# Seven-product chunks of the down projection: product order, order of the sums, and which chunks use them

## The chip, the cores and the metric

One core of one Trainium2 chip. The number is the device time in microseconds (us) of one launch. The kernel before takes 1178.64 us, the median of 3 runs (1177.26 to 1179.37).

## The reference

One decoder layer on x of 256 tokens by 2048 features, all in float32:

```
proj = x @ W_in                                   # 2048 x 6144
a    = diff_attention(...), b = moba_attention(...)
h    = LayerNorm(alpha * x + concat(a, b) @ W_out)
u    = h @ W_up                                   # 2048 x 11264: gate g and value v, 5632 each
act  = silu(conv_b + causal_conv3(g)) * v         # 256 x 5632
out  = LayerNorm(alpha * h + act @ W_down)        # W_down: 5632 x 2048
```

Only the last product, act @ W_down, and the second LayerNorm's sums are touched by the change.

## The kernel before, in words

Every float32 operand of a matmul is split into a rounded part `hi` (ScalarE copies it to fp32r) and a rest `lo` (VectorE subtracts). A product is then three matmuls: hi by hi, hi by lo, lo by hi. Weights come as a stream of chunks of 128 x 2048 numbers (1 MB) through four buffers `raw`; chunk i + 6 is loaded by SyncE's queue when chunk i begins (`load`). `begin(i)`, `middle(i)` and the matmuls of chunk i are written out chunk after chunk, and each engine runs its own instructions in just that order. So the text of `begin` and `middle` is the queue of ScalarE (ACT) and VectorE (DVE): `begin(i)` prepares chunk i + 2 (second half) and the activations of i + 1 and i + 2, `middle(i)` prepares the first half of chunk i + 3.

The down projection runs in two column passes n = 0 and 1, each over 22 chunks p (two of the 44 rows-of-128 of W_down, 1024 of its columns). The chunk is a 2 x 2 block problem: the two 128-token halves t, the two row blocks k, the two blocks c of 512 columns. A normal chunk (`mm_d`) makes 8 block products of three matmuls with 512 columns, 24 matmuls, into four PSUM banks `CB[t][c]`. A seven-product chunk (`mm_seven`, a Strassen-Winograd form) makes 7 block products, 21 matmuls. It needs sums of activation blocks (`act_sums`, split in `act_sums_split` into `sh`, `sl`) and of weight blocks, and its split weights lie in one tile `slot` of 7 blocks: blocks 0 to 2 are raw (unsummed), blocks 3 to 6 are sums. The rest of blocks 0 to 2 is made by ACT writing the negative rounded part and then a DMA from POOL's queue that adds the raw numbers on top (`blocks_raw`, line 517). Blocks 3 and 4 get their rest in `blocks_lo`, blocks 5 and 6 in `blocks_sum`. Four products go to banks of their own, `MB[1], MB[5], MB[6], MB[7]`, which are added to the result z once a pass in `shared_out`.

Before, the seven-product chunks (`SEVEN`, line 45) are p = 2, 5, 8, 11, 14, 17, 20 in pass 0 and 1, 4, 7, 10, 13, 16 in pass 1: 13 in all, two normal chunks between any two. The tile `slot` exists once. The split activations `ah, al` (k = 0) and `bh, bl` (k = 1) have so few buffers that the copies at the head of `begin(i)` wait until the matmuls of chunk i - 1 are done.

The last four chunks of pass 1 (`last`) aren't run chunk by chunk: they go column block by column block, so that LayerNorm can begin early. Two of them have split weights in tiles of their own, `end0` and `end1`, made in the bodies of the two chunks ahead (lines 906 to 916). `gb` (2 MB, scale and offset of the last LayerNorm) is loaded at p = 9 of pass 1 (line 905). At the end of pass 0 the banks `CB` are added to z by `z_piece`, which also takes the LayerNorm statistics of each piece (line 400), at lines 924 to 934; the next pass writes the same banks.

Of the kernel before, what the change touches and what calls it, by code (L numbers as in the profile page):

```python
# [11 lines left out]
F32 = mybir.dt.float32  # L12
F32R = mybir.dt.float32r
AF = mybir.ActivationFunctionType
ALU = mybir.AluOpType

P = 128
D = 2048
# [11 lines left out]
ALPHA = 2.0 ** 0.25  # L30
# [11 lines left out]
PAIRED_END = 4  # L42
PT = FT // 2

SEVEN = (range(2, PT, 3), range(1, PT - PAIRED_END, 3))

ENDS = {(1, 1): ("cos_d", "sin_d"), (2, 0): ("mask", "cos_m"), (2, 1): ("sin_m", "lam4")}

# [2 lines left out]
def hymba_layer(ctx: ExitStack, tc: tile.TileContext, a: dict):  # L51
# [72 lines left out]
    def split(i, half, both=None):  # L124

        if i >= NS or (i, half) in parts:
            return
        t = loaded[i] if half == 0 else loaded.pop(i)
        if both is None:
            hi = splits.tile([P, 1024], F32R, name="hi")  # L130
            lo = splits.tile([P, 1024], F32R, name="lo")
        else:
            hi, lo = both[:, half], both[:, 2 + half]
        for x, y in pieces(i, half):
            if i < 4 and x % 512 == 0:
                split_x(4 * i + x // 512, 4 * i + (y + 511) // 512)
            s = slice(x - 1024 * half, y - 1024 * half)
            ACT.activation(hi[:, s], t[:, x:y], AF.Copy)  # L138
            DVE.tensor_tensor(lo[:, s], t[:, x:y], hi[:, s].bitcast(F32), ALU.subtract)  # L139
        parts[i, half] = (hi, lo)  # L140
# [101 lines left out]
    def at(step, fn, *args, rank=LATER):  # L242
        after.setdefault(step, []).append((rank, len(after.get(step, ())), fn, args))
# [210 lines left out]
    def seven(i):  # L454
        return stream[i][0] == "d" and stream[i][1] in SEVEN[stream[i][2]]

# [16 lines left out]
    def split_act(i, k):  # L473

        if i >= NS or stream[i][0] != "d" or (i, k) in aparts:
            return
        src = act_of(2 * stream[i][1] + k)
        hi, lo = act_tiles(i, k)
        ACT.activation(hi, src, AF.Copy)
        DVE.tensor_tensor(lo, src, hi.bitcast(F32), ALU.subtract)  # L480
        aparts[i, k] = (hi, lo)
# [5 lines left out]
    def act_sums(i):  # L487
        p = stream[i][1]
        x = [act_of(2 * p + k) for k in range(2)]
        a11, a21, a12, a22 = (x[k][:, t * P:(t + 1) * P] for k in range(2) for t in range(2))  # L490
        f = [keep.tile([P, 2, P], F32, name="sf", tag=g) for g in ("cos_d", "sin_d")]
        DVE.tensor_tensor(f[0][:, 0], a21, a11, ALU.subtract)
        DVE.tensor_tensor(f[0][:, 1], a22, a21, ALU.subtract)
        DVE.tensor_tensor(f[1][:, 0], f[0][:, 1], a11, ALU.add)
        DVE.tensor_tensor(f[1][:, 1], a12, f[1][:, 0], ALU.subtract)
        sums[i] = f

    def act_sums_split(i):
        f = sums[i]
        out = []  # L500
        for j in range(2):
            hi = keep.tile([P, 2, P], F32R, name="sh", tag=("mask", "cos_m")[j])
            lo = keep.tile([P, 2, P], F32R, name="sl", tag=("sin_m", "lam4")[j])
            ACT.activation(hi, f[j], AF.Copy)  # L504
            DVE.tensor_tensor(lo, f[j], hi.bitcast(F32), ALU.subtract)
            out += [(hi[:, k], lo[:, k]) for k in range(2)]

        sums[i] = out
# [3 lines left out]
    def blocks_raw(i):  # L512

        t = loaded[i].rearrange("p (b c) -> p b c", c=512)
        slot = keep.tile([P, 2, 7, 512], F32R, name="slot", tag="t2")
        ACT.activation(slot[:, 1, 0:3], t[:, 0:3], AF.Copy, scale=-1.0)
        POOL.dma_start(slot[:, 1, 0:3], t[:, 0:3], accum_op=ALU.add)
        f = [work.tile([P, 512], F32, name="tf", tag="m1") for _ in range(2)]
        DVE.tensor_tensor(f[0], t[:, 0], t[:, 3], ALU.subtract)
        DVE.tensor_tensor(f[1], t[:, 3], t[:, 2], ALU.add)  # L520
        blocks[i] = (slot, f)
        for j in range(2):
            ACT.activation(slot[:, 0, 3 + j], f[j], AF.Copy)
        ACT.activation(slot[:, 0, 0:3], t[:, 0:3], AF.Copy)

    def blocks_lo(i):
        slot, f = blocks[i]
        for j in range(2):
            DVE.tensor_tensor(slot[:, 1, 3 + j], f[j], slot[:, 0, 3 + j].bitcast(F32), ALU.subtract)  # L529

    def blocks_sum(i, j):

        t = loaded[i].rearrange("p (b c) -> p b c", c=512)
        slot, f = blocks[i]
        DVE.tensor_tensor(f[0], t[:, 2 - j], f[0], ALU.subtract)  # L535
        ACT.activation(slot[:, 0, 5 + j], f[0], AF.Copy)  # L536
        DVE.tensor_tensor(slot[:, 1, 5 + j], f[0], slot[:, 0, 5 + j].bitcast(F32), ALU.subtract)
        if j == 1:
            loaded.pop(i)


    idle = keep.tile([P, 512], mybir.dt.bfloat16, name="idle")
# [12 lines left out]
    def begin(i):  # L555

        urgent(i)
        j = i + 2
        split_act(j - 1, 1)
        split_act(j, 0)  # L560
        if j < NS and seven(j):
            blocks_raw(j)
        else:
            split(j, 1)
        if j - 1 < NS and seven(j - 1):
            blocks_sum(j - 1, 1)
            act_sums_split(j - 1)
        load(i + 6)
        pending(i)

    def middle(i):

        urgent(i + 0.5)
        if i + 2 < NS and seven(i + 2):
            blocks_lo(i + 2)
            act_sums(i + 2)
            blocks_sum(i + 2, 0)
        if i + 3 < NS and not seven(i + 3):
            split(i + 3, 0)
        pending(i + 0.5)  # L580

# [264 lines left out]
    def mm_seven(i):  # L846
        n = stream[i][2]
        slot, _ = blocks.pop(i)
        s3, s1, s2, s4 = sums.pop(i)
        (h0, l0), (h1, l1) = aparts[i, 0], aparts[i, 1]  # L850
        a11, a12, a22 = (h0[:, 0:P], l0[:, 0:P]), (h1[:, 0:P], l1[:, 0:P]), (h1[:, P:], l1[:, P:])
        for m, lhs, b in ((5, s1, 3), (7, s3, 4), (6, s2, 5), (1, a11, 0), (2, a12, 1), (3, s4, 2), (4, a22, 6)):
            t, c = {2: (0, 0), 3: (0, 1), 4: (1, 0)}.get(m, (None, None))
            key, dst = ((n, m), MB[m]) if t is None else ((n, t, c), CB[t][c])
            if m == 6:
                middle(i)
            mm_three(key, dst, lhs, (slot[:, 0, b], slot[:, 1, b]))

    def z_add(n, t, c, src, alpha=1.0):
        s = slice((2 * n + c) * 512, (2 * n + c + 1) * 512)  # L860
        DVE.scalar_tensor_tensor(z[:, t, s], z[:, t, s], alpha, src, op0=ALU.mult, op1=ALU.add)  # L861

    def shared_out(n):

        u = acts[2][:, 12:14].rearrange("p a b -> p (a b)")
        ACT.activation(u, MB[1], AF.Copy)
        z_add(n, 0, 0, u, ALPHA)
        DVE.tensor_tensor(u, MB[6], u, ALU.add)
        z_add(n, 0, 1, MB[5], ALPHA)
        z_add(n, 0, 1, u)  # L870
        DVE.tensor_tensor(u, MB[7], u, ALU.add)
        z_add(n, 1, 1, MB[5], ALPHA)
        z_add(n, 1, 0, u, ALPHA)
        z_add(n, 1, 1, u)

    last = range(NS - PAIRED_END, NS)

# [23 lines left out]
    for i in range(first_d, NS - PAIRED_END):  # L901
        begin(i)
        _, p, n, _ = stream[i]
        if n == 1 and p == 9:
            load_gb(2, keep.tile([P, 2, D], F32, name="gb2", tag="ma"))
        if i == last[0] - 2:
            end1 = keep.tile([P, 4, 1024], F32R, name="end1", tag="mb")
            split(last[3], 0, end1)
            split(last[3], 1, end1)
        if i == last[0] - 1:  # L910
            end0 = keep.tile([P, 4, 1024], F32R, name="end0", tag="t2")
            split(last[2], 0, end0)
            split(last[2], 1, end0)
            for j in last[1:]:
                for k in range(2):
                    split_act(j, k)
        if seven(i):
            mm_seven(i)
            if p == SEVEN[n][-1]:
                at(i + 1, shared_out, n)  # L920
        else:
            for k in range(2):
                mm_d(i, 0, [0, 1], k)
            if n == 0 and p == PT - 1:
                for c in range(2):
                    z_piece(0, c, CB[0][c], 2, alpha=1.0)
            if i < last[0] - 1:
                middle(i)
            for k in range(2):
                mm_d(i, 1, [0, 1], k)  # L930
            done(i)
            if n == 0 and p == PT - 1:
                for c in range(4):
                    z_piece(1, c, CB[1][c // 2][:, c % 2 * 256:c % 2 * 256 + 256], 2, 256, 1.0)
        for k in range(2):
            aparts.pop((i, k))

# [132 lines left out]
```

## Time and profile before

| | |
|---|---|
| median of 3 runs | 1178.64 us |
| profiled execution's own time | 1178.97 us |
| its span in the trace | 1177.1 us |
| granted clock of TensorE, mean | 0.986 |
| first matmul of the down projection | 888.33 us |
| last matmul | 1165.95 us |

Times in the rows are microseconds from the start of the span. PE is TensorE (PEld its weight loads), DVE VectorE, ACT ScalarE, POOL GpSimd, SP SyncE (with a q behind the name: its queue). A timeline row is: start, length, engine, line, operation, the tile written and the tiles read, shapes, how many instructions are merged (x2), and in brackets the idle time of the engine just before and what ended it. Matmuls overlap in the pipeline, so the step from one start to the next is what a matmul costs, not its length; DVE and ACT instructions overlap by about 0.1 us in the same way.

### The profile page before, as it was taken

How to read it: one execution, taken by the hardware profiler on the slowest of the kernel's cores; microseconds unless marked ns; L12 is line 12 of the kernel's file. 1: busy time of each engine (PE TensorE's matmuls, PEld its weight loads, DVE VectorE, ACT ScalarE, POOL GpSimd, SP SyncE). 2: the span in 40 equal slices, each digit the busy share in tenths (PEclk: the TensorE clock that was granted, in tenths of full speed). 3: DMA queues.
4: the chain of work that ended last, by engine and by line, in shares of the span. 5: the costliest groups of instructions: out<-in, count | busy, mean ns of one | idle time of the engine just before them, and what ended most of it. 6: DMA issues, size and time to landing. Idle time of an engine off the chain costs nothing.

```text
span 1177.1 us, 15646 instructions
## 1 busy us (share of the span) xinstructions
PE 1136.3 (97%) x5965; PEld 962.7 (82%) x5965; DVE 822.5 (70%) x1399; ACT 622.7 (53%) x1019; POOL 32.0 (3%) x40
## 2 busy tenths in 40 slices
PE   9999999999999999999999999999999999789976
PEld 6888888888888888888888888888887777567755
DVE  6886877858646777776566666666667877777774
ACT  6565555444434565455454455455456666456641
POOL 0000000000000000000000000000000000000004
PEclk9999999999999999999999999999999999889988
DMA  9665454444555285555554555555556778467921
GB/s 340 256 242 181 157 179 173 159 171 178 179 178 184 103 321 182 202 189 179 197 195 181 190 200 183 184 200 189 183 185 199 209 217 259 142 188 215 330 81 72
DMA packets 47611, 228.13 MB, mean 194 GB/s; under 512 B 4656, under 2 KB 6576, under 8 KB 27952
## 3 DMA queue, kind: packets, MB, share of 16 engines
q1 hardware_dynamic: 45664, 216.92, 51.9%
q0 software_dynamic: 1872, 10.22, 4.3%
q8 instruction: 46, 0.75, 0.3%
q14 instruction: 29, 0.24, 0.1%
HBM read 214.80 MB, written 2.10 MB: 184 GB/s over the span
## 4 chain that ended last, share of the span: by engine, by line
PE 87%; DVE 6%; issue 2%; ACT 2%; DMA 1%; SPq 0%; POOL 0%; ACTq 0%; DVEq 0%
PE bank L206 87%; DVE lo L139 2%; ACT hi L138 1%; DVE tf L535 1%; DVE z L861 1%; DMA raw<-in_w_d 1%; DVE bl L480 0%; PE bank L329 0%; DVE al L480 0%; DMA raw<-in_w_v 0%; ACT sh L504 0%; DVE end L139 0%; DVE st L400 0%; DVE z L397 0%; DVE slot L529 0%
## 5 line engine op out<-in xcount | busy, mean ns | idle before, releaser
L139 DVE TENSOR_TENSOR lo<-raw,hi 128x1024 fp32r<-128x1024 f32 (+1 forms) x368 | 436.0, 1200 | 206.8 <-ACT hi L138 206.3
L138 ACT ACTIVATE hi<-raw 128x1024 fp32r<-128x1024 f32 (+1 forms) x368 | 375.9, 1034 | 214.6 <-PE bank L206 187.0
L206 PE MATMUL bank<-h,hi 128*128 128x512 f32 x1376 | 477.2, 390 | 0.0
L206 PE MATMUL bank<-h,lo 128*128 128x256 f32 x1376 | 388.0, 282 | 0.0
L206 PEld LDWEIGHTS bank<-h,hi 128*128 128x128 f32 x1376 | 258.3, 188 | 54.1
L206 PEld LDWEIGHTS bank<-h,lo 128*128 128x128 f32 x1376 | 260.1, 189 | 0.0
L206 PE MATMUL bank<-x,hi 128*128 128x512 f32 x512 | 181.6, 396 | 0.0
L206 PE MATMUL bank<-x,lo 128*128 128x256 f32 x512 | 144.3, 282 | 0.0
L206 PEld LDWEIGHTS bank<-x,hi 128*128 128x128 f32 x512 | 96.1, 188 | 21.7 <-issue 1.3
L206 PEld LDWEIGHTS bank<-x,lo 128*128 128x128 f32 x512 | 96.8, 189 | 0.2
L206 PE MATMUL bank<-hi,x 128*128 128x512 f32 x256 | 85.3, 402 | 0.7 <-ACT hi L138 0.7
L206 PEld LDWEIGHTS bank<-hi,x 128*128 128x128 f32 x256 | 48.1, 188 | 13.2 <-ACT hi L138 1.9
L443 ACT ACTIVATE gc<-gs,vec 128x256 f32<-128x256 f32 x43 | 25.9, 602 | 58.6 <-DVE gs L220 58.6
L206 PE MATMUL bank<-lo,x 128*128 128x512 f32 x128 | 50.8, 397 | 0.4 <-DVE lo L139 0.4
L206 PE MATMUL bank<-hi,ah 128*128 128x512 f32 (+1 forms) x118 | 39.2, 404 | 9.6 <-DVE z L397 9.6
L536 ACT ACTIVATE slot<-tf 128x512 fp32r<-128x512 f32 x26 | 16.4, 632 | 55.1 <-DVE tf L535 55.1
L206 PE MATMUL bank<-slot,sh 128*128 128x512 f32 x104 | 35.0, 419 | 9.6 <-ACT sh L504 9.6
L446 ACT ACTIVATE gc<-gc 128x256 f32<-128x256 f32 x44 | 18.4, 418 | 48.9 <-DVE gc L445 48.9
L206 PE MATMUL bank<-hi,mh 128*128 128x512 f32 x128 | 42.1, 400 | 0.0
L206 PE MATMUL bank<-lo,mh 128*128 128x512 f32 x128 | 41.6, 395 | 0.0
L206 PE MATMUL bank<-hi,ml 128*128 128x512 f32 x128 | 41.6, 395 | 0.0
L444 DVE SCALAR_TENSOR_TENSOR gc<-gs,vec,gc 128x255 f32<-128x255 f32 x43 | 20.8, 484 | 28.8 <-ACT gc L443 28.8
(176 smaller groups left out, 1355.8 us busy)
## 6 DMA issues: line engine op xcount, KB each, us to landing
raw<-in_w_u SPq DMA_DIRECT2D x88, 1024.0 KB, 4.8
raw<-in_w_d SPq DMA_DIRECT2D x88, 512.0 KB, 5.3
raw<-in_w_qk SPq DMA_DIRECT2D x32, 1024.0 KB, 4.9
raw<-in_w_o SPq DMA_DIRECT2D x16, 1024.0 KB, 4.8
raw<-in_w_v SPq DMA_DIRECT2D x12, 1024.0 KB, 4.8
slot<-raw POOLq DMA_DIRECT2D x13, 768.0 KB, 6.5
raw<-in_w_v SPq DMA_DIRECT2D x8, 256.0 KB, 4.7
raw<-in_w_v SPq DMA_DIRECT2D x4, 512.0 KB, 7.6
```

What stands on the lines that cost most here:

```text
L138: ACT.activation(hi[:, s], t[:, x:y], AF.Copy)
L139: DVE.tensor_tensor(lo[:, s], t[:, x:y], hi[:, s].bitcast(F32), ALU.subtract)
L206: PE.matmul(out, lhsT, rhs, start=start, stop=stop)
L443: ACT.activation(gc, g, AF.Identity, bias=vec[:, C_CB + f:C_CB + f + 1], scale=w[2])
L444: DVE.scalar_tensor_tensor(gc[:, 1:], g[:, 0:S - 1], w[1], gc[:, 1:], op0=ALU.mult, op1=ALU.add)
L446: ACT.activation(gc, gc, AF.Silu)
L535: DVE.tensor_tensor(f[0], t[:, 2 - j], f[0], ALU.subtract)
L536: ACT.activation(slot[:, 0, 5 + j], f[0], AF.Copy)
L861: DVE.scalar_tensor_tensor(z[:, t, s], z[:, t, s], alpha, src, op0=ALU.mult, op1=ALU.add)
```

## The change

The set of seven-product chunks becomes p = 3, 6, 9, 12, 15, 18 in pass 0 and 1, 4, 7, 10, 13 in pass 1: 11 instead of 13. Within such a chunk the products of raw block 0 and raw block 1 come first. For a seven-product chunk c the preparation is laid out anew: in `begin(c-2)` the activation sums follow `blocks_raw`; in `middle(c-2)` the order is rest of block 3, sum for block 5, rest of block 4, split of the activation sums, rounded block 5, first half of chunk c + 1, rest of block 5; in `begin(c-1)` it is sum for block 6, second half of chunk c + 1, rounded block 6, rest of block 6. `shared_out` is cut in two, run one and two chunks after the last seven-product chunk of the pass. At the end of pass 0 the banks are added to z in whole 512-column pieces without statistics, and the statistics (`z_stats`) follow in `begin` of chunks 1 and 2 of pass 1. The own tiles of the two last chunks are both made in the body of the chunk just ahead of the last four.

```
-SEVEN = (range(2, PT, 3), range(1, PT - PAIRED_END, 3))
+SEVEN = (range(3, 19, 3), range(1, 14, 3))
...
-    def blocks_lo(i):
+    def blocks_lo(i, *js):
         slot, f = blocks[i]
-        for j in range(2):
-            DVE.tensor_tensor(slot[:, 1, 3 + j], f[j], slot[:, 0, 3 + j].bitcast(F32), ALU.subtract)
+        for j in js:
+            DVE.tensor_tensor(slot[:, 1, 3 + j], f[j % 2 if j < 2 else 0], slot[:, 0, 3 + j].bitcast(F32),
+                              ALU.subtract)
...                                                             # blocks_sum(i, j):
         DVE.tensor_tensor(f[0], t[:, 2 - j], f[0], ALU.subtract)
-        ACT.activation(slot[:, 0, 5 + j], f[0], AF.Copy)
-        DVE.tensor_tensor(slot[:, 1, 5 + j], f[0], slot[:, 0, 5 + j].bitcast(F32), ALU.subtract)
         if j == 1:
             loaded.pop(i)
+
+    def blocks_hi(i, j):
+        slot, f = blocks[i]
+        ACT.activation(slot[:, 0, 5 + j], f[0], AF.Copy)
...                                                             # begin(i), j = i + 2:
         if j < NS and seven(j):
             blocks_raw(j)
+            act_sums(j)
+        elif j - 1 < NS and seven(j - 1):
+            blocks_sum(j - 1, 1)
+            split(j, 1)
+            blocks_hi(j - 1, 1)
+            blocks_lo(j - 1, 3)
         else:
             split(j, 1)
-        if j - 1 < NS and seven(j - 1):
-            blocks_sum(j - 1, 1)
-            act_sums_split(j - 1)
...                                                             # middle(i):
         if i + 2 < NS and seven(i + 2):
-            blocks_lo(i + 2)
-            act_sums(i + 2)
+            blocks_lo(i + 2, 0)
             blocks_sum(i + 2, 0)
-        if i + 3 < NS and not seven(i + 3):
+            blocks_lo(i + 2, 1)
+            act_sums_split(i + 2)
+            blocks_hi(i + 2, 0)
+            split(i + 3, 0)
+            blocks_lo(i + 2, 2)
+        elif i + 3 < NS and not seven(i + 3):
             split(i + 3, 0)
...                                                             # mm_seven:
-        for m, lhs, b in ((5, s1, 3), (7, s3, 4), (6, s2, 5), (1, a11, 0), (2, a12, 1), (3, s4, 2), (4, a22, 6)):
+        for m, lhs, b in ((1, a11, 0), (2, a12, 1), (5, s1, 3), (7, s3, 4), (6, s2, 5), (3, s4, 2), (4, a22, 6)):
...
+    def shared_out(n, part):
         u = acts[2][:, 12:14].rearrange("p a b -> p (a b)")
+        if part == 0:
+            ACT.activation(u, MB[1], AF.Copy)
+            z_add(n, 0, 1, MB[5], ALPHA)
+            z_add(n, 1, 1, MB[5], ALPHA)
+            z_add(n, 0, 0, u, ALPHA)
+            DVE.tensor_tensor(u, MB[6], u, ALU.add)
+        else:
+            z_add(n, 0, 1, u)
+            DVE.tensor_tensor(u, MB[7], u, ALU.add)
+            z_add(n, 1, 0, u, ALPHA)
+            z_add(n, 1, 1, u)
...                                                             # the loop over chunks:
-        if i == last[0] - 2:
-            end1 = keep.tile([P, 4, 1024], F32R, name="end1", tag="mb")
-            split(last[3], 0, end1)
-            split(last[3], 1, end1)
         if i == last[0] - 1:
-            end0 = keep.tile([P, 4, 1024], F32R, name="end0", tag="t2")
-            split(last[2], 0, end0)
-            split(last[2], 1, end0)
-            for j in last[1:]:
+            split_act(last[1], 1)
+            for j, g in ((last[2], "t2"), (last[3], "mb")):
+                end = keep.tile([P, 4, 1024], F32R, name="end", tag=g)
                 for k in range(2):
                     split_act(j, k)
+                    split(j, k, end)
...
             if p == SEVEN[n][-1]:
-                at(i + 1, shared_out, n)
+                at(i + 1, shared_out, n, 0)
+                at(i + 2, shared_out, n, 1)
...                                                             # p = 21 of pass 0, ahead of middle(i):
-                    z_piece(0, c, CB[0][c], 2, alpha=1.0)
+                    z_add(0, 0, c, CB[0][c])
...                                                             # and behind its matmuls:
-                for c in range(4):
-                    z_piece(1, c, CB[1][c // 2][:, c % 2 * 256:c % 2 * 256 + 256], 2, 256, 1.0)
+                for c in range(2):
+                    z_add(0, 1, c, CB[1][c])
+                for t in range(2):
+                    for c in range(2):
+                        at(i + 2 + t, z_stats, t, c, (512, 256)[t])
```

`z_stats(t, c, w)` runs the `bn_stats` instructions of one piece of 512 columns, in widths w.

## Rows read from the trace of the kernel before

**Rows 1.** The page: busy time, share of the span and instructions of each engine.
```profile
PE 1136.3 (97%) x5965; PEld 962.7 (82%) x5965; DVE 822.5 (70%) x1399; ACT 622.7 (53%) x1019; POOL 32.0 (3%) x40
```

**Rows 2.** One stretch: bounds, length, busy per engine, granted clock, DMA share, GB/s.
```profile
931.00:948.00 17.00, 16.25 (x69) 12.62 (x69) 13.42 (x24) 11.39 (x18) 0.86 (x1) 1.00 0.76 228
```

**Rows 3.** Waits of PE from 888 us on: total us, times, longest.
```profile
PE bank L206 <- DVE z L397: 9.6, 4, 5.4
PE bank L206 <- ACT sh L504: 9.6, 12, 1.7
PE bank L206 <- DVE eh L480: 6.2, 1, 6.2
```

**Rows 4.** Timeline of PE over the down projection.
```profile
888.33 0.62 PE L206 MATMUL bank<-hi,ah 128*128 128x512 f32 x2
...
901.26 0.73 PE L206 MATMUL bank<-slot,sh 128*128 128x512 f32 x2 [1.72 <-ACT sh L504]
...
920.01 0.74 PE L206 MATMUL bank<-slot,sh 128*128 128x512 f32 x2 [0.72 <-ACT sh L504]
...
922.49 0.62 PE L206 MATMUL bank<-slot,ah 128*128 128x512 f32 x2
...
925.28 0.63 PE L206 MATMUL bank<-hi,ah 128*128 128x512 f32 x2
...
930.82 0.64 PE L206 MATMUL bank<-hi,ah 128*128 128x512 f32 x2
...
1006.13 0.73 PE L206 MATMUL bank<-slot,sh 128*128 128x512 f32 x2 [0.71 <-ACT sh L504]
...
1022.47 0.76 PE L206 MATMUL bank<-hi,ah 128*128 128x512 f32 x1 [5.37 <-DVE z L397]
...
1037.68 0.99 PE L206 MATMUL bank<-slot,sh 128*128 128x512 f32 x2
...
1123.77 0.73 PE L206 MATMUL bank<-slot,sh 128*128 128x512 f32 x2 [0.72 <-ACT sh L504]
...
1144.82 0.79 PE L206 MATMUL bank<-hi,eh 128*128 128x512 f32 x1 [6.23 <-DVE eh L480]
...
1149.25 0.39 PE L206 MATMUL bank<-hi,ah 128*128 128x512 f32 x1
...
1165.95 0.28 PE L206 MATMUL bank<-end,cl 128*128 128x256 f32 x1
```

**Rows 5.** Timeline of ACT and DVE between two seven-product chunks.
```profile
908.08 0.42 ACT L479 ACTIVATE bh<-act 128x256 fp32r<-128x256 f32 x1 [4.06 <-PE bank L206]
908.53 0.43 DVE L480 TENSOR_TENSOR bl<-act,bh 128x256 fp32r<-128x256 f32 x1 [3.00 <-ACT bh L479]
908.71 1.47 ACT L516 ACTIVATE slot<-raw 128x1536 fp32r<-128x1536 f32 x1
910.74 1.29 DVE L529 TENSOR_TENSOR slot<-tf,slot 128x512 fp32r<-128x512 f32 x2 [0.24 <-ACT slot L523]
911.13 1.48 ACT L524 ACTIVATE slot<-raw 128x1536 fp32r<-128x1536 f32 x1
911.95 0.29 DVE L492 TENSOR_TENSOR sf<-act 128x128 f32<-128x128 f32 x1
...
917.16 1.22 DVE L139 TENSOR_TENSOR lo<-raw,hi 128x1024 fp32r<-128x1024 f32 x1
918.29 0.69 DVE L535 TENSOR_TENSOR tf<-raw,tf 128x512 f32<-128x512 f32 x1
```

**Rows 6.** Timeline of DVE at the end of pass 0.
```profile
1020.44 1.29 DVE L861 SCALAR_TENSOR_TENSOR z<-z,act 128x512 f32<-128x512 f32 x2
```

**Rows 7.** The adding DMA: issue, landing of all 13, landing in 1096:1112.
```profile
910.50 0.88 POOL L517 DMA_DIRECT2D slot<-raw  x1 [18.23 <-DMA raw<-in_w_d]
DMA to landing us min/median/max: 5.7/6.5/10.2
slot<-raw POOLq DMA_DIRECT2D x1, 768.0 KB, 10.2
```

More of the change, by code (lines that the diff above doesn't have):

```diff
@@ L524, in blocks_raw @@
         ACT.activation(slot[:, 0, 0:3], t[:, 0:3], AF.Copy)
-    def blocks_lo(i):
+    def blocks_lo(i, *js):
         slot, f = blocks[i]
-        for j in range(2):
-            DVE.tensor_tensor(slot[:, 1, 3 + j], f[j], slot[:, 0, 3 + j].bitcast(F32), ALU.subtract)
+        for j in js:
+            DVE.tensor_tensor(slot[:, 1, 3 + j], f[j % 2 if j < 2 else 0], slot[:, 0, 3 + j].bitcast(F32),
+                              ALU.subtract)
     def blocks_sum(i, j):
         t = loaded[i].rearrange("p (b c) -> p b c", c=512)
-        slot, f = blocks[i]
+        f = blocks[i][1]
         DVE.tensor_tensor(f[0], t[:, 2 - j], f[0], ALU.subtract)
-        ACT.activation(slot[:, 0, 5 + j], f[0], AF.Copy)
-        DVE.tensor_tensor(slot[:, 1, 5 + j], f[0], slot[:, 0, 5 + j].bitcast(F32), ALU.subtract)
         if j == 1:
             loaded.pop(i)
+    def blocks_hi(i, j):
+        slot, f = blocks[i]
+        ACT.activation(slot[:, 0, 5 + j], f[0], AF.Copy)
     idle = keep.tile([P, 512], mybir.dt.bfloat16, name="idle")
@@ L861, in z_add, with z_stats @@
         DVE.scalar_tensor_tensor(z[:, t, s], z[:, t, s], alpha, src, op0=ALU.mult, op1=ALU.add)
-    def shared_out(n):
+    def shared_out(n, part):
         u = acts[2][:, 12:14].rearrange("p a b -> p (a b)")
[L866 to L874, printed above, removed]
+        if part == 0:
[9 more added lines that the diff above has]
+            z_add(n, 1, 1, u)
+    def z_stats(t, c, w):
+        if (2, t) not in stats:
+            stats[2, t] = work.tile([P, D // w, 6], F32, name=f"st{w}")
+        for j in range(512 // w):
+            DVE.bn_stats(stats[2, t][:, c * 512 // w + j], z[:, t, c * 512 + j * w:c * 512 + (j + 1) * w])
     last = range(NS - PAIRED_END, NS)
```

## The prediction

> **What bounds the kernel now.** First the page: PE is busy 97% of the span [rows 1], so the kernel looks done. But a busy PE may run at half clock, and the first 888 us of the span are not changed. So the down projection is read by itself, from its first matmul at 888.33 to its last at 1165.95 [rows 4]. Next one stretch of it: in 17 us PE is busy 16.25, DVE 13.42, ACT 11.39, the DMA engines 0.76, at granted clock 1.00 [rows 2]. No helper is full; PE waits by order, not by load. The waits name three places [rows 3]: ACT's `sh` before each seven-product chunk (12 times, 9.6 us), DVE's z at the end of pass 0 (9.6), DVE's `eh` at the end (6.2).
>
> The waits understate the loss, because the clock falls behind them. So I compare with the pace of undisturbed stretches. A normal chunk takes 930.82 - 925.28 = 5.54; twelve matmuls of a seven-product chunk take 925.28 - 922.49 = 2.79, so its 21 take 4.88 [rows 4]. Three chunks should take 15.96. What each stretch takes above that, by its first and last row [rows 4]:
>
> - start, 888.33 to 901.26, two normal chunks: 12.93 - 11.08 = 1.85
> - first three chunks, 901.26 to 920.01: 18.75 - 15.96 = 2.79
> - 920.01 to 1006.13, five rounds of three: 86.12 - 79.80 = 6.32
> - end of pass 0, 1006.13 to 1037.68, one round: 31.55 - 15.96 = 15.59
> - 1037.68 to 1123.77, five rounds: 86.09 - 79.80 = 6.29
> - 1123.77 to 1149.25, a seven-product chunk, a normal one and the first column block of the last four (24 matmuls, 5.58): 25.48 - 16.00 = 9.48
>
> Together 42.3 us lost. From 1149.25 on nothing is lost: the 16.70 to the last matmul are three times the pace of the first column block. The loss of a stall is its idle time and a stretch at half clock: the first round costs 18.75 and the later ones 17.22, and what the first has more, 1.5, is the price of the fall behind its 1.72 us of waiting; behind 0.72 there is no such excess. I use 1.5 per fall.
>
> **The change part by part.** *Fewer seven-product chunks.* Two of 13 become normal: 2 x (5.54 - 4.88) = +1.3, on PE, which is the path.
>
> *The round of three.* Let T be the end of a seven-product chunk on PE; c is the next one, and PE reaches it at T + 11.1. At T ACT's copy `bh` is released (908.08) and DVE follows 0.45 later [rows 5]. All the work is the same as before; only its order differs. A 512-column DVE operation takes 0.6 (two in 1.29, with overlap), a 1024-column one 1.13 (917.16 to 918.29), the small splits 0.34, an activation sum 0.29 [rows 5]. ACT: small copies, negative block, two block copies, then the raw blocks, done at 911.13 + 1.48 = T + 4.5 [rows 5]. DVE in the new order: two small splits to T + 1.1, two block sums 2.3, four activation sums 3.5, rest 3, sum 5, rest 4 to 5.3, the two `sl` 6.0. ACT meanwhile copies `sh` to 5.2, block 5 to 5.8, the half of c + 1 to 6.8; so DVE's 1024-column rest of it runs to 8.0, rest 5 to 8.6. Then `begin(c-1)`: small splits 9.3, sum 6 9.9, 1024-column rest 11.0, rest 6 11.6; `middle(c-1)` 12.8; `begin(c)` small splits and a 1024-column rest 14.6. PE needs `sl` at 11.1 + 6 x 0.2325 (third product now) and has it at 6.0; block 6 at 11.1 + 18 x 0.2325 = 15.3 and has it at 11.6. DVE is free at 14.6, 1.3 before PE ends c at 15.96. So the wait on `sh` goes, and ACT and DVE get no new one. What is late next: the DMA that adds the raw blocks, now wanted by the second matmul. Its bound from below is no wait: issued at T + 2.4, median landing 6.5 [rows 5, 7], at T + 8.9 against 11.3. From above: landing in 10.2 [rows 7], a wait of 1.3. That one row lies behind the 2 MB load of `gb`; I take no wait in all rounds but that one (p = 13), and there 1.3 to 2.1 (the loads now follow each other some 1 us more closely), say 1.5, with 1.0 for the clock between none and 1.5: 2.5 in all.
>
> SP's loads are moved with their releases: chunk c + 4 waits for the sums of c, now done at T + 9.9, c + 5 for T + 11.0, c + 6 for T + 14.6. Each is wanted by ACT over 5 us after it lands. The DMA share becomes 0.76 x 17 / 15.96 = 0.81 [rows 2]: cover enough; without it a round would wait for its raw.
>
> *Start.* The first seven-product chunk is p = 3, so its preparation begins one chunk later, when DVE has the last activation behind it. One more half chunk of rests (1.13) moves ahead of p = 0; DVE is done near 892.6, before T = 893.9. Loss 0 in place of 4.64; if the cover fails, one more wait as now, 1.85.
>
> *End of pass 0.* The last seven-product chunk is p = 18; call its end A. DVE then: `begin(19)` and the first part of `shared_out` (small splits, 1.13, three adds and a sum at 0.6 to 0.7, by [rows 6]) to A + 5.5; `middle(19)` waits for PE at 5.54, since six split halves are in use, to 7.8; `begin(20)` 9.6, second part 12.3; `begin(21)` with block and activation sums 15.2; two adds of z 16.4; `middle(21)`: rest, sum, rest 18.2, `sl` 19.0, the 1024-column rest behind ACT 20.5, rest 5 21.1; then z's second row 21.8 and 22.4. PE ends p = 21 at A + 16.6 and the first half of the next chunk at 19.4; its banks `CB[1]` come free at 21.9 and 22.5. PE stands 2.9 and the clock falls once: 4.4. The statistics (1.2 and 1.4 of DVE) come a round later, in the 1.3 that DVE has over, so at nothing; without that cover about 1. Bounds: 0 (were z's adds ahead of `middle`) to 9 (the old stall of 5.37 [rows 4] and two and a half falls).
>
> *End of pass 1.* Four normal chunks 14 to 17 now lie between the last seven-product chunk (end B) and the last four. By the same sums `shared_out` is done at B + 12.3, DVE's work for the first two of the last four at 21, for the third at 24, for the fourth at 26.9; PE wants them at B + 22.2, 23.6, 25.0 and 26.4, of the fourth only the first half, done at 25.4. The raw of the fourth is issued at B + 9.7 and wanted at 20. Loss 0 for 9.48; from above half of the 6.23 of now [rows 4], 3.
>
> *Sum.* -42.3 + 1.3 + 2.5 + 4.4 = -34.1. From the profiled execution's 1178.97 that is 1144.9; the median is 0.3 less. I forecast 1145.
>
> **The rivals.**
>
> A. As summed: 1145, its own range 1140 to 1151 by the bounds of the two stalls.
>
> B. No stall is left: -42.3 + 1.3 = -41.0, 1138. For it: the bound of zero in each part. Against it: DVE's queue at the end of pass 0 has 22 us of work in 19.4.
>
> C. The round isn't freed: each keeps 0.6 to 1.26 of its loss, since ACT and DVE alternate and every hand-over costs a little more than I count. Ten rounds: +6 to +12.6, 1151 to 1157. For it: DVE is free only 1.3 before it is wanted. Against: what PE itself waits for is early by 2.5 (the split of a12, at 9.3 for 11.8), 3.7 (block 6) and more.
>
> D. The adding DMA is late in every round by what that one row shows: 1.3 and a fall of 1.5, 2.8 x 10 = 28, 1173. For it: a round shrinks from 17.22 to 15.96, so the third load, issued at T + 14.6, comes 1.3 nearer to the next adding DMA, and the DMA engines rise from 0.76 to 0.81. Against: a median of 6.5 with the DMA engines at 0.76, and over 2 us in hand. The page "DMA: Bandwidth & Descriptors" of the Trainium skill, section "Queues, rings and completion order", says that a DMA engine takes the queues it has work for in turns, packet by packet; by that the adding DMA shares each engine whenever loads stand in SP's queue, and D would hold if they always did. The 10.2 beside the `gb` load agrees with it, the median of 6.5 says that it is not the common case.
>
> E. Slower than before, by the same mechanism further on: the raw blocks come first, so every microsecond of a late landing now stands before PE. The gain of 34.1 + 2.5 spread on 11 chunks is 3.3 each; less the fall of 1.5 that is a wait of 1.8, a landing 10.7 after its issue. Above that in every chunk the change loses; at 12 us it is 11 x (3.1 + 1.5) = 50.6, 1144.9 - 2.5 + 50.6 = 1193. No landing in the rows is that long.
>
> F. The change does not do what it says, as some wait on the tile as a whole (`slot` written by four engines) holds PE until block 6 is done: T + 11.6 against 11.1, 0.5 each, so within C; no change in sum would need all stalls to stay: 1178 to 1180.
>
> **How the numbers follow.** A 0.65, B 0.09, C 0.15, D 0.05, E 0.04, F as no change 0.02. The range 1139 to 1155 holds A, half of B and most of C. A measurement of this kernel can tell about 0.2%, 2.4 us, from no change. A to D are faster: 0.94; same 0.02; slower 0.04.
>
> **What would show it.** Right: seven-product chunks 15.9 to 16.1 apart with no wait on `sh`; no half clock near 901; one wait on z of 2 to 3.5 near the start of pass 1, first t = 1 matmul; `bl` of ACT's head still released by PE; a short wait on the adding DMA at p = 13 alone; no wait for `eh`; last matmul near 1132. Wrong: waits for DMA before the second matmul of every such chunk (D, E), waits on DVE inside the round (C), or a second fall of the clock at the end of pass 0.

## The result, and the profile after

The changed kernel takes 1144.06 us (median of 4 runs, 1143.47 to 1144.30); the kernel before, beside it, 1179.01 (1177.26 to 1179.88). The ratio is 0.9705, 95% interval 0.9688 to 0.9721. The profiled execution took 1144.30, with a span of 1142.5. Forecast: 1145, within 1139 to 1155.

The page of the changed kernel, the line that answers to [rows 1] and the granted clock in 40 slices:

```profile
PE 1124.0 (98%) x5971; PEld 961.2 (84%) x5971; DVE 810.2 (71%) x1373; ACT 614.6 (54%) x1007; POOL 30.2 (3%) x38
...
PEclk9999999999999999999999999999999999999998
```

The waits of PE from 888 us on, as in [rows 3]:

```profile
PE bank L206 <- DVE z L871: 2.3, 1, 2.3
...
PE bank L206 <- DMA slot<-raw: 1.7, 2, 1.3
```

`sh` and `eh` are gone from the list; z has one wait left of four, and the adding DMA is new. PE's timeline at the places of [rows 4]:

```profile
889.36 0.62 PE L206 MATMUL bank<-hi,ah 128*128 128x512 f32 x2
...
905.95 0.63 PE L206 MATMUL bank<-slot,ah 128*128 128x512 f32 x2
...
921.91 0.63 PE L206 MATMUL bank<-slot,ah 128*128 128x512 f32 x2
...
985.86 0.63 PE L206 MATMUL bank<-slot,ah 128*128 128x512 f32 x2
...
1012.62 1.09 PE L206 MATMUL bank<-hi,ah 128*128 128x512 f32 x2 [2.35 <-DVE z L871]
...
1015.85 0.63 PE L206 MATMUL bank<-slot,ah 128*128 128x512 f32 x2
...
1048.60 0.50 PE L206 MATMUL bank<-slot,ah 128*128 128x512 f32 x1 [0.43 <-DMA slot<-raw]
...
1080.39 0.40 PE L206 MATMUL bank<-slot,ah 128*128 128x512 f32 x1
...
1082.08 0.50 PE L206 MATMUL bank<-slot,ah 128*128 128x512 f32 x1 [1.28 <-DMA slot<-raw]
...
1108.97 0.40 PE L206 MATMUL bank<-hi,ah 128*128 128x512 f32 x1
...
1131.28 0.28 PE L206 MATMUL bank<-end,cl 128*128 128x256 f32 x1
```

Held against the same pace (5.54, 4.88, 5.58) the stretches lose: three chunks to 905.95, 16.59 for 16.62, nothing; five rounds to 985.86, 79.91 for 79.80, 0.1; a seven-product and four normal chunks to 1015.85, 29.99 for 27.04, 2.95; four rounds to 1080.39, 64.54 for 63.84, 0.7; the last seven-product and four normal chunks to 1108.97, 28.58 for 27.04, 1.54; the rest nothing. Together 5.3 in place of 42.3. With +1.3 for two chunks more of the normal kind, and the down projection beginning at 889.36 instead of 888.33, the change is -42.3 + 5.3 + 1.3 + 1.0 = -34.7, which is 1144.3 - 1178.97. The 1.0 isn't the change's: the same shift stands already near 400 us (that stage's one wait of PE ends at 399.25 before, 400.27 after), in code that both kernels share, and in the kernels below the down projection begins anywhere from 887.79 to 889.31.

### The profile page after: what moved, and what is told of

Same layout as the page of the kernel before. It is cut to its first block, busy times and chain, and to the rows that moved or that the text cites. A ratio compares the mean times of both kernels' runs of the same rounds, so it can differ in the third digit from the quotient of the medians.

```text
span 1142.5 us, 15605 instructions
## 1 busy us (share of the span) xinstructions
PE 1124.0 (98%) x5971; PEld 961.2 (84%) x5971; DVE 810.2 (71%) x1373; ACT 614.6 (54%) x1007; POOL 30.2 (3%) x38
## 4 chain that ended last, share of the span: by engine, by line
PE 93%; DMA 3%; DVE 2%; ACT 1%; issue 0%; SPq 0%; POOL 0%; ACTq 0%
PE bank L206 92%; DMA slot<-raw 2%; DMA raw<-in_w_v 1%; PE bank L329 0%; DVE z L871 0%; DVE lo L139 0%; ACT slot L516 0%; ACT hi L138 0%; DVE z L976 0%; PE bank L705 0%; SPq L155 0%; PE bank L376 0%; SPq L121 0%; ACT hf L708 0%; DVE h L720 0%
## 5 line engine op out<-in xcount | busy, mean ns | idle before, releaser
L139 DVE TENSOR_TENSOR lo<-raw,hi 128x1024 fp32r<-128x1024 f32 (+1 forms) x372 | 440.8, 1200 | 216.5 <-ACT hi L138 216.2
L138 ACT ACTIVATE hi<-raw 128x1024 fp32r<-128x1024 f32 (+1 forms) x372 | 380.1, 1035 | 230.0 <-PE bank L206 198.3
L206 PE MATMUL bank<-lo,ah 128*128 128x512 f32 (+1 forms) x126 | 39.7, 390 | 0.0
L206 PE MATMUL bank<-hi,al 128*128 128x512 f32 (+1 forms) x126 | 39.7, 390 | 0.0
```

The source lines that it names most:

```text
L206: PE.matmul(out, lhsT, rhs, start=start, stop=stop)
```

## The experiments

Each kernel's time is a median, beside runs of the kernel before on the same chip (1178.66 for the first four, 1178.48 for the second four).

**The set alone, and the rest alone.** `e1_set_only` is the kernel before with one line of the change:

```
-SEVEN = (range(2, PT, 3), range(1, PT - PAIRED_END, 3))
+SEVEN = (range(3, 19, 3), range(1, 14, 3))
```

> The kernel before with only the set of seven-product chunks changed (3, 6, ..., 18 and 1, 4, ..., 13); order of the sums, of the products, of z and of the last splits as before. Theory (order of ACT's and DVE's queues makes the wait inside a round, the place of the chunks makes those at the ends of the passes): the rounds keep 1.26 each, ten of them, the start and the end of pass 1 are freed, the end of pass 0 keeps 2 to 4 more than the changed kernel since the statistics lie in DVE's queue there; the two waits for the adding DMA go: 1144.1 + 12.6 + 3 - 2 = 1158, 1154 to 1163. Rival (two chunks fewer take enough work from DVE, the order matters little): 1145 to 1148.

Measured: 1158.51, ratio 0.9834 (0.9821 to 0.9848). `e2_order_only` is the changed kernel with the old line, and `at(i + 2 - n, shared_out, n, 1)` for the second part. It adds that part in pass 0 after the direct products of one block, so this block is scaled by ALPHA with them and the output isn't the layer's; the instructions are of the same kind and number, and only the time is read.

> The changed kernel with the old set of 13 seven-product chunks (2, 5, ..., 20 and 1, 4, ..., 16); the second part of the shared sums of pass 1 comes one chunk after its last one, as there is no later one. Theory: rounds stay at 15.9 to 16.1, the start loses nothing much either (preparation of p = 2 done 3 us ahead), 1.3 is won by two more seven-product chunks, but the end of pass 0 gets the shared sums next to its z adds (4 to 6 more) and the end of pass 1 gets late loads and the shared sums before the last splits (6 to 8 more): 1153, 1147 to 1159. Rival (the set did it): 1165 or more.

Measured: 1149.77, ratio 0.9759 (0.9746 to 0.9772). Waits in the timeline of PE, `e1_set_only` (the first row here is one of ten waits on `sh`: 0.44 before the first seven-product chunk, 0.71 to 0.99 before the others; only the one after the end of pass 0 has none):

```profile
922.19 0.73 PE L206 MATMUL bank<-slot,sh 128*128 128x512 f32 x2 [0.72 <-ACT sh L504]
...
1020.02 0.79 PE L206 MATMUL bank<-hi,ah 128*128 128x512 f32 x1 [3.89 <-DVE z L397]
1021.58 0.80 PE L206 MATMUL bank<-hi,ah 128*128 128x512 f32 x1 [0.77 <-DVE z L397]
...
1125.68 0.50 PE L206 MATMUL bank<-hi,eh 128*128 128x512 f32 x1 [0.98 <-DVE eh L480]
```

and `e2_order_only`, all of them in the down projection:

```profile
1007.20 1.08 PE L206 MATMUL bank<-hi,ah 128*128 128x512 f32 x2 [1.52 <-DVE z L871]
1013.11 1.34 PE L206 MATMUL bank<-hi,ah 128*128 128x512 f32 x2 [2.54 <-DVE z L871]
1083.85 0.50 PE L206 MATMUL bank<-slot,ah 128*128 128x512 f32 x1 [1.38 <-DMA slot<-raw]
1113.21 0.50 PE L206 MATMUL bank<-hi,eh 128*128 128x512 f32 x1 [0.38 <-DVE eh L480]
1114.68 1.41 PE L206 MATMUL bank<-end,eh 128*128 128x512 f32 x5 [0.74 <-DVE end L139]
1117.62 0.73 PE L206 MATMUL bank<-end,dhl 128*128 128x512 f32 x2 [1.29 <-DVE end L139]
```

With the set alone the wait on `sh` stays at ten of the eleven chunks; with the orders alone it is gone in every round, and the waits stand at the ends of the passes, but for one on the adding DMA (p = 13 of pass 1). Both parts are needed for the whole, and they overlap: the set alone is worth 20.2 of the 34.6, the orders alone 28.9. The start is freed by the orders (no wait at all at p = 2 in the second list) and nearly by the set (0.44 is left of 1.72), so it is in both sums. Both times lie in their ranges, but not each part: against the same pace, the end of pass 0 in `e1_set_only` cost 4.8 more than in the changed kernel where 2 to 4 was expected, and the end of pass 1 in `e2_order_only` lost 3.2 where 6 to 8 was expected.

**Which order in the round.** `e3_sums_first` puts the products back in their old order in the changed kernel:

```
-((1, a11, 0), (2, a12, 1), (5, s1, 3), (7, s3, 4), (6, s2, 5), (3, s4, 2), (4, a22, 6))
+((5, s1, 3), (7, s3, 4), (6, s2, 5), (1, a11, 0), (2, a12, 1), (3, s4, 2), (4, a22, 6))
```

> The changed kernel with the old order of the seven products (the three with summed blocks first, raw blocks fourth and fifth). Theory (the new order of DVE's queue has the sums split 5 us ahead, so the product order isn't what removed the wait; it only moves the adding DMA's deadline 2.1 us earlier): no wait for the sums comes back, the two waits of PE for the adding DMA (0.6 at p = 7, 1.5 at p = 13 of pass 1) go: 1142.0, 1141.3 to 1143. Rival (the raw products first cover the sums' lateness): each of ten rounds gets 0.7 to 1.3 back, 1151 to 1157.

Measured: 1142.56, ratio 0.9696 (0.9683 to 0.9710). The interval overlaps with the changed kernel's, so the time alone says only that nothing is lost. The waits of PE from 885 us on say more, this is all of them:

```profile
PE bank L206 <- DVE z L871: 2.3, 1, 2.3
```

and the DMA landed no sooner (first row) than in the changed kernel (second row):

```profile
DMA to landing us min/median/max: 5.8/7.2/10.7
...
DMA to landing us min/median/max: 5.7/7.3/10.3
```

So the new place of the raw products did not remove the wait on `sh`. The new order of the preparation in ACT's and DVE's queues did: `e1_set_only`, with the same set and the old order, has the wait at nearly every such chunk. Which move within that order is needed was not tried apart. Raw products first only bring the adding DMA's deadline forward, and that cost the two waits of the changed kernel.

**The load beside the adding DMA.** `e4_gb_late`:

```
-        if n == 1 and p == 9:
+        if n == 1 and p == 13:
```

> The changed kernel with the load of scale and offset (2 MB) at p = 13 of pass 1 instead of p = 9, behind the last adding DMA. Theory (the wait of 1.28 at p = 13 is the adding DMA sharing the DMA engines with that load): the wait at p = 13 goes, the 0.4 at p = 7 stays: 1142.6, 1142 to 1143.3. Rival (the DMA is late because rounds are shorter and loads closer, whatever the 2 MB load does): 1144.1, unchanged.

Measured: 1143.54, ratio 0.9700 (0.9687 to 0.9714); again not apart from the changed kernel in time, and 0.2 above the theory's range. The profile shows where the gain went: from its chunk 18 of pass 0 to chunk 1 of pass 1 this execution takes 31.57, the changed kernel's 29.99, with the same wait on z but a fall of the clock behind it (more on that below). The landings of `e4_gb_late`:

```profile
DMA to landing us min/median/max: 5.8/6.8/8.8
```

The longest fell from 10.3 to 8.8 and no wait on the adding DMA is left, at p = 13 as expected, at p = 7 too, where I expected it to stay: that one, a landing of 9.4 in the changed kernel's profile, is absent here (an 8.8 in this kernel cost nothing). The traces bear the theory out at p = 13: all four kernels with raw products first, a seven-product chunk there and the load at p = 9 wait for the adding DMA at that chunk, 1.28 in the changed kernel, 1.38 in `e2_order_only`, 1.30 in `e6_z_old`, 1.22 in `e7_end_old`. The load isn't the only cause of a late landing: see the next kernel.

**The end of pass 0.** `e5_pass1_from_2` takes the preparation out of the place where z is added:

```
-SEVEN = (range(3, 19, 3), range(1, 14, 3))
+SEVEN = (range(3, 19, 3), range(2, 15, 3))
...
-        if n == 1 and p == 9:
+        if n == 1 and p == 13:
```

> The changed kernel with the seven-product chunks of pass 1 at 2, 5, 8, 11, 14 instead of 1, 4, 7, 10, 13, and the 2 MB load at p = 13. Theory (the wait left at the end of pass 0 is DVE's queue: the preparation of chunk 1 lies between the last chunk of pass 0 and its z adds): with the preparation one chunk later DVE has z's second row at A + 17.9 where PE wants it at 19.4, the wait of 2.35 and the half-speed pair behind it go (-2.95); with the load moved no wait for the adding DMA at the end (-1.5): 1139.6, 1138.8 to 1141. At the other end one normal chunk less lies ahead of the last four; DVE's sums give 1.3 to spare there. Rival (the z adds are late anyway, or the wait moves to the last splits): 1142.5 to 1145.

`e6_z_old` puts the old pieces with their statistics back (`z_piece` in place of `z_add` at both places, without `z_stats`).

> The changed kernel with the end of pass 0 as before: z's pieces with their statistics at once, second row in pieces of 256. Theory (all that lies in DVE's queue ahead of z's second row is paid by PE there): two statistics (1.2) ahead, then pieces with statistics instead of two adds, +0.9 to the first bank and +1.5 to the second: 2.7 more of waiting, 1146.8; with a fall of the clock behind the longer wait 1148.3. Range 1146 to 1149. Rival (statistics fit in DVE's spare time anyway): 1144.

Measured: `e5_pass1_from_2` 1138.77, ratio 0.9662 (0.9649 to 0.9675); `e6_z_old` 1148.25, ratio 0.9742 (0.9729 to 0.9755). The first is 0.03 below its range, the second at the value forecast with a fall of the clock. The only wait of PE in the first one's down projection, and its landings:

```profile
1035.44 0.50 PE L206 MATMUL bank<-slot,ah 128*128 128x512 f32 x1 [0.88 <-DMA slot<-raw]
...
DMA to landing us min/median/max: 6.1/7.1/9.9
```

This wait was not foreseen. It is at p = 5, eight chunks ahead of the 2 MB load, and the landing of 9.9 is that chunk's; what made it late is not shown.

The waits at the end of pass 0 in the second:

```profile
1007.51 0.47 PE L206 MATMUL bank<-hi,ah 128*128 128x512 f32 x1 [0.27 <-DVE z L397]
1014.05 0.79 PE L206 MATMUL bank<-hi,ah 128*128 128x512 f32 x1 [3.73 <-DVE z L397]
1015.61 0.80 PE L206 MATMUL bank<-hi,ah 128*128 128x512 f32 x1 [0.77 <-DVE z L397]
```

with the clock behind them (`e6_z_old`; bounds, length, busy per engine, granted clock, DMA share, GB/s):

```profile
1014.00:1018.00 4.00, 3.18 (x7) 2.19 (x8) 3.90 (x9) 0.69 (x2) 0.00 (x0) 0.50 0.02 4
```

So what lies ahead of z's second row in DVE's queue is what PE waits for there: take the preparation away and the wait is gone, put the statistics back and the waits that the rows show go from 2.35 to 4.77 in all, with a stretch at half clock behind them. The "half-speed pair" of the expectation for `e5_pass1_from_2` was a misreading; the part on the end of pass 0 below says what it is.

**The last splits.** `e7_end_old` keeps the changed kernel but makes `end0` and `end1` as before, activations last.

```
-            for j, g in ((last[2], "t2"), (last[3], "mb")):
-                end = keep.tile([P, 4, 1024], F32R, name="end", tag=g)
...
+        if i == last[0] - 2:
+            end1 = keep.tile([P, 4, 1024], F32R, name="end1", tag="mb")
...
+            end0 = keep.tile([P, 4, 1024], F32R, name="end0", tag="t2")
```

> The changed kernel with the own tiles of the last two chunks made as before (one in the body of each of the two chunks ahead, activations last). Theory (the end of pass 1 was freed by the place of the last seven-product chunk, not by the order of the last splits): DVE's sums put the activations of the last three at B + 24.3 to 25.6, wanted at 24.3 to 26.4, so at most a wait of 0.5 to 1: 1144.7, 1144 to 1146. Rival (the new order of the last splits frees the end): 4 or more back, 1148 to 1153.

Measured: 1145.33, ratio 0.9718 (0.9705 to 0.9731). No wait of PE at the end of pass 1; the two waits it has are two of the changed kernel's three:

```profile
1012.50 1.31 PE L206 MATMUL bank<-hi,ah 128*128 128x512 f32 x2 [2.34 <-DVE z L871]
1083.01 0.50 PE L206 MATMUL bank<-slot,ah 128*128 128x512 f32 x1 [1.22 <-DMA slot<-raw]
```

So the new order of the last splits isn't needed: without it the end is free. The place of the last seven-product chunk frees most of it and so do the new orders: of 7.2 of waiting before, 0.98 is left with the new place and the old order of everything (`e1_set_only`), 2.41 with the new orders and the old place (`e2_order_only`). In time this kernel's interval overlaps with the changed one's. In the profiled executions its down projection takes 243.18 for 241.92, and the stretch from chunk 18 of pass 0 to chunk 1 of pass 1, with the fall of the clock shown below, alone takes 1.59 more.

**All three together.** `e8_both`: sums first, pass 1 at 2, 5, ..., 14, and the 2 MB load at p = 14.

> Three edits together on the changed kernel: sums first in the product order, seven-product chunks of pass 1 at 2, 5, 8, 11, 14, the 2 MB load at p = 14. Theory: no wait of PE is left in the down projection; by the count of matmuls 1144.1 less the 5.3 that the changed kernel still loses: 1138.8, 1138 to 1140. Rival (the old product order starts a seven-product chunk on blocks that come later, and with DVE's statistics in the same round the sums are late once or twice): 1140 to 1142.

Measured: 1137.90 (1137.53 to 1138.96), ratio 0.9657 (0.9644 to 0.9670), clear of the changed kernel's interval, so faster than that; from `e5_pass1_from_2` it isn't apart. It is 0.1 below its range. From its first matmul of the down projection to its last, without one wait of PE:

```profile
888.03 0.62 PE L206 MATMUL bank<-hi,ah 128*128 128x512 f32 x2
...
1124.55 0.28 PE L206 MATMUL bank<-end,cl 128*128 128x256 f32 x1
```

That is 236.5; the count of matmuls at the undisturbed pace gives 16 x 5.54 + 6 x 4.88 for pass 0, 13 x 5.54 + 5 x 4.88 + 5.58 + 16.70 for pass 1, 236.6. Rival B's 1138 is what this kernel shows, by an order that the change does not have.

## Why the prediction was right, point by point

*The loss of 42.3.* Right as a measure: `e8_both` runs the whole down projection at the undisturbed pace, so all of it was there to be won.

*The round of three.* Right in each step, within 0.2. ACT's `bh` is released at 926.82 in the changed kernel (T), then in DVE and ACT, in order of time:

```profile
926.82 0.42 ACT L479 ACTIVATE bh<-act 128x256 fp32r<-128x256 f32 x1 [3.00 <-PE bank L206]
...
932.14 0.76 DVE L505 TENSOR_TENSOR sl<-sf,sh 128x256 fp32r<-128x256 f32 x2
...
937.62 0.68 DVE L529 TENSOR_TENSOR slot<-tf,slot 128x512 fp32r<-128x512 f32 x1
...
940.03 1.22 DVE L139 TENSOR_TENSOR lo<-raw,hi 128x1024 fp32r<-128x1024 f32 x1
```

`sl` is done at T + 6.1 (worked out: 6.0), the rest of block 6 at 11.5 (11.6), the last of the round at 14.4 (14.6). Rounds are 15.96 to 16.07 apart, but for the one with the wait at p = 7. Rival C and rival F have nothing on their side: no wait on DVE or ACT inside a round.

*The adding DMA.* Mechanism right, size over: 1.28 of waiting at p = 13 was forecast at 1.5, the fall of the clock that I charged at 1.0 did not come (the step from 1080.39 to 1108.97 loses 1.54 in all), and 0.7 was lost at p = 7, which I had at nothing; so the sign "at p = 13 alone" failed. 2.5 was taken, 2.2 came. Rival D had the right place and too high a frequency: two of 11 chunks waited. Moving the 2 MB load moves the longest landing from 10.3 to 8.8 (`e4_gb_late`); the median of 7.3, with 8.9 in hand, says that most landings pass freely. The Trainium skill's rule that a DMA engine takes its queues in turns ("DMA: Bandwidth & Descriptors", "Queues, rings and completion order") agrees with the first of these numbers. The landing of 10.7 from which rival E decides was reached by one DMA of `e3_sums_first`, where the old product order hid it.

*Start.* Right: no loss (16.59 for 16.62).

*End of pass 0.* The queue was right to about a tenth. The end of p = 18 is A = 990.74 (ACT's next `bh` starts at 990.77); DVE's adds of z's second row and what is ahead of them:

```profile
1001.75 1.29 DVE L871 SCALAR_TENSOR_TENSOR z<-z,act 128x512 f32<-128x512 f32 x2
...
1009.01 0.76 DVE L505 TENSOR_TENSOR sl<-sf,sh 128x256 fp32r<-128x256 f32 x2
1010.14 1.23 DVE L139 TENSOR_TENSOR lo<-raw,hi 128x1024 fp32r<-128x1024 f32 x1 [0.37 <-ACT hi L138]
1011.28 0.68 DVE L529 TENSOR_TENSOR slot<-tf,slot 128x512 fp32r<-128x512 f32 x1
1011.89 1.28 DVE L871 SCALAR_TENSOR_TENSOR z<-z,bank 128x512 f32<-128x512 f32 x2
```

They end at A + 22.4 (22.4), PE goes on at A + 21.9 (21.9), 2.35 late. Its first two matmuls then go to the two banks, one behind each add: the second can start only after the second add ends at 1013.17, so the pair takes 0.93 instead of 0.47, at full clock (the changed kernel; bounds, length, busy per engine, granted clock, DMA share, GB/s):

```profile
1012.60:1013.60 1.00, 0.88 (x3) 0.53 (x4) 1.00 (x3) 0.00 (x0) 0.00 (x0) 1.00 0.00 0
```

The stretch loses 2.95 in all, the 2.9 of standing still that was forecast. The term of the sum that was mis-sized is the fall of the clock, 1.5, which this execution did not pay: 2.95 for a forecast of 4.4. It is a matter of the execution: `e3_sums_first`, `e4_gb_late` and `e7_end_old` wait the same 2.34 to 2.35 there, and in them the clock falls. The four us behind the wait in `e7_end_old`:

```profile
1014.00:1018.00 4.00, 4.00 (x13) 3.12 (x12) 3.60 (x6) 2.48 (x5) 0.00 (x0) 0.67 0.58 154
```

and in the changed kernel:

```profile
1014.00:1018.00 4.00, 4.00 (x19) 3.26 (x18) 4.00 (x7) 3.15 (x5) 0.00 (x0) 1.00 0.58 149
```

13 matmuls for 19 in 4 us: six times 0.23, or 1.4, close to the 1.5 that I had charged.

*End of pass 1.* Right: no wait. By `e7_end_old` it needs the place of the last seven-product chunk and the new orders ahead of it, not the new order of the last splits.

*Sum.* Forecast -34.1, came -34.7. The losses left were 1.6 smaller than forecast (5.3 for 6.9, the two falls of the clock less the wait at p = 7), and the 1.0 by which the down projection began later in this execution took most of that back. So the mechanism was right in the main, and that the sum came within 0.6 is luck in part: whether the clock falls differs from one execution to the next, and the late start has nothing to do with the change.

## What to carry to other kernels

Before a kernel whose main engine is 97% busy is called done, hold each stage against its own undisturbed pace: 42 us of 278 were lost here, of which PE's waits showed only 26 (the three of [rows 3] and 1.0 on ACT's `eh`). Where helpers have time over on average, write their queues out with durations from the trace and compare each result's time with its first use; one late result is mended by order, and what lay in DVE's queue ahead of the bank that PE wanted next was paid by PE (`e5_pass1_from_2`, `e6_z_old`). A product order that uses a slow DMA's data first spends slack that another order keeps for nothing.

## What the runs showed of the hardware that I had not expected

The fall of TensorE's clock behind a wait isn't fixed by the wait's length. 2.34 to 2.35 us at one and the same place left the granted clock at 1.00 in one execution (the changed kernel), and at a mean of 0.65 to 0.74 over the stretch from 1014 to 1018 in three others (`e4_gb_late`, `e7_end_old`, `e3_sums_first`). A shorter wait, the 1.72 that ended at 901.26 in the kernel before, was followed by half clock:

```profile
903.00:905.00 2.00, 2.00 (x6) 1.57 (x5) 2.00 (x4) 1.02 (x2) 0.00 (x0) 0.50 1.00 398
```

Behind 3.73 and 0.77 (`e6_z_old`) it was 0.50, the lower of the two levels, throughout 4 us; behind the 1.28 at p = 13 there was no fall (1.00 from 1082 to 1088).
